# Five blocks of activations are turned by 32x32 stream transposes and a store and load, in place of TensorE transposes

## The chip, the cores and the metric

The kernel runs on one core of a Trainium2 chip. The metric is the device time of one execution in microseconds (us). The engines are named as in the profile: PE is TensorE (matmuls), PEld its weight loads, DVE is VectorE, ACT is ScalarE, POOL is GpSimd, SP is SyncE, which only issues DMAs. Each engine runs its own queue of instructions in a fixed order, and waits at an instruction until what it needs is there.

## The reference

A two-layer decoder trunk on 256 tokens of width 2048, all in float32. Layer 0 is a pooling mixer and a SwiGLU FFN; then one set of keys and values is made from the stream; layer 1 is attention over that set, and a SwiGLU FFN. Every sub-layer takes a normed and modulated stream. Cut to the two places that the change touches:

```python
def modulate(h, shift, scale):
    return h * (1.0 + scale[:, None, :]) + shift[:, None, :]
...
h = modulate(rmsnorm(x, norm_mix[1]), shift_m, scale_m)      # layer 1, the mixer's input
cq = rmsnorm(h @ w_dq, q_norm)                               # the queries' latent
q = (cq @ w_uq).reshape(B, S, N_HEADS, Q_HEAD_DIM)
...
x = x + gate_m[:, None, :] * y
h = modulate(rmsnorm(x, norm_ffn[1]), shift_f, scale_f)      # layer 1, the FFN's input
x = x + gate_f[:, None, :] * ((silu(h @ w_gate) * (h @ w_up)) @ w_down)
```

## The kernel before

**Products in three parts.** A float32 product is made from three matmuls of a reduced-precision type: each operand is split into an upper half (a rounded copy, ACT) and a lower half (the rest, by subtraction, DVE), and upper x upper, lower x upper and upper x lower are summed in PSUM. A weight unit is 512 x 512. `w_unit` (L384) loads it from DRAM on SP's queue into a `raw` buffer (six of them), and `split` (L372) makes its halves in two `hl` buffers (six): L376 on ACT, L378 on DVE. `proj_unit` (L412, its matmul is L422) multiplies one unit with one block of activations, for two groups of 128 tokens: 24 matmuls.

**Activations.** A block of activations is 512 channels of the normed, modulated stream for all 256 tokens, with the channels along the partitions, both halves in an `act` buffer. The stream itself (`x`) has tokens along the partitions, so a block has to be turned. `scaled` (L546) multiplies 512 columns of `x` by each token's reciprocal norm (ACT, L554), one piece for each group of 128 tokens. `turned_pieces` (L558) turns them by eight transposes on PE (L564) into two PSUM banks. `modulated` (L571) applies scale and shift, which are per channel and so per partition now: for each of four groups of 128 channels ACT writes the whole value (L582) and its upper half (L583), and DVE the lower half (L584). The pieces and the whole values lie in `t2k` buffers, of which there are seven.

**Background.** The modulation vectors come from products of a vector with large matrices. They are made on DVE in the background (`Part.unit`: a load of 1 MB on SP's queue, a multiply-and-sum L213), a few units at a time: `plan` and `release` set how many are to be done in a stage, and `tick`, called by each `split`, spreads them.

**The order.** Outside the stretches that are marked as ordered by hand, a planner sets each engine's queue when the kernel is built: work that is ready goes in the order of the program, and a later instruction goes first only where nothing earlier is ready on that engine. The two halves of a weight's split are given a priority as if they stood 100 instructions earlier; instructions under `urgent` (L588) go as early as they can. A buffer is given out when an instruction that writes it is placed.

**The queries' latent.** After FFN 0, keys and values are made in four groups (`keys_values`, L1367; `head_T`'s matmul is L1386). The pieces of the first block are scaled before group 1. In group 2, between its keys and its values, `last_of_background` (L1403) first places what is left of the stage's background and then calls `hidden_q` (L1396), which turns block 0, scales block 1 and modulates block 0. After group 2 `hidden_q` turns and modulates block 1. Blocks 2 and 3 need no turning: they were kept, turned, from the keys' and values' own norm. Then follow a few DVE additions that complete the rotary key (`rope_end`, L912, into `krT`, which GpSimd clears at L1413), the four units of `w_dq` with blocks 0 to 3 in that order, `Latent.norm` with a power on GpSimd (L1338), and group 3.

**The last FFN.** `start_ffn` (L930) begins the first six of eleven column chunks of both projections before all blocks are there: for each block j it runs over twelve units (six chunks, gate and up) with that block, for block 0 without the first two, which the handover from the attention has done. In the loop over the units, n counts 0 to 11; `pieces = ahead(j + 1)` scales the next block behind unit n = 7, and `hidden(j + 1, pieces)` turns and modulates it ahead of unit n = 11. Block 0 is made in the handover, blocks 1 to 3 in this way.

**An earlier use of the other way.** In both FFNs some chunks of the product of gate and up are already turned without PE: `turn_blocks` (L748) turns each 32x32 block in place (L752, a stream transpose on DVE) and stores the tile to DRAM (L754, on POOL's queue), and `transposed` (L764) loads it with partition and block index exchanged (L769, POOL's queue). What results has its channels in another order than PE's transpose gives, and the rows of the weights that meet it are laid out on the host in that order (`laid_out`, L1718).

Of the kernel before, what the change touches and what calls it, by code (L numbers as in the profile page):

```python
# [17 lines left out]
P = 128  # L18
# [77 lines left out]
def tile_trunk(ctx: ExitStack, tc: tile.TileContext, a: dict, out: bass.AP):  # L96
# [22 lines left out]
    def t2k(shape, dt=F32):  # L119
        return work.tile(shape, dt, tag="t2k", bufs=7, name=nm("t2k"))  # L120
# [437 lines left out]
    def turned_pieces(pieces):  # L558
# [7 lines left out]
            pts.append(pt)  # L566
        return pts

    mod_ins, hid_ins = [None], [None]

    def modulated(pts, j, c_scale, c_shift, direct=False):  # L571
        flush()
# [165 lines left out]
    def ffn(l, hT, gate_name, begun, then):  # L738
# [7 lines left out]
            return proj(ffn_weights(l)[which][:, c], hT)  # L746

        def turn_blocks(c):  # L748
            turned[c] = []
            for tok in range(NT):  # L750
                blocks = t2k([P, CH])
                dve.transpose(out=blocks, in_=nat[c][tok])  # L752
                rows = dram.tile([P, CH], F32, name=nm("turned"))
                pool.dma_start(rows, blocks)  # L754
                turned[c].append(rows)

        def turned_halves(m, tok, full):
            order = "p k (b j) -> p k b j"
# [5 lines left out]
        def transposed(c):  # L764
            m = act_t([P, 2, KL, T])
            if c in TURNED_BY_DMA[l]:
                for tok in range(NT):
                    full = t2k([P, CH])
                    pool.dma_start(full.rearrange("p (b e) -> p b e", e=P),  # L769
                                   turned[c][tok].rearrange("(b i) (g e) -> (i g) b e", i=BLOCK, e=P))  # L770
                    halves = lambda tok=tok, full=full: turned_halves(m, tok, full)
                    if c == GROUPS[-1][0]:
                        halves()
                    else:
                        pending.append((1, halves))
                mids[c] = m
                return
            for tok in range(NT):
                pt = ps_t()
                for f in range(KL):  # L780
                    pe.transpose(pt[:, f * P:(f + 1) * P], nat[c][tok][:, f * P:(f + 1) * P], ident)  # L781
                v = pt.rearrange("p (f t) -> p f t", f=KL)
                ts_ = slice(tok * P, (tok + 1) * P)
                act.activation(m[:, 0, :, ts_], v, AF.Copy)
                dve.tensor_tensor(out=m[:, 1, :, ts_], in0=v, in1=m[:, 0, :, ts_].bitcast(F32), op=ALU.subtract)
            mids[c] = m
# [143 lines left out]
    def start_ffn(l, first, ahead, hidden, late):  # L930
# [3 lines left out]
        with tc.issue_after(mod_ins[0].ins), tc.issue_after(hid_ins[0].ins) if hid_ins[0] else nullcontext():  # L934
            for j in range(ND - 1):
                if l == 0 and j == 1:
                    for tok in range(NT):
                        sync.dma_start(aside[0][:, tok], back[tok])
                todo = KD // 2 if j + 1 >= ND - late else 0
                for n, (c, which) in enumerate((c, w) for c in begun for w in (GATE, UP)):  # L940
                    if n == 2 * len(begun) - 1:
                        hT.append(hidden(j + 1, pieces))
                    if l == 0 or j > 0 or c > 0:
                        begun[c][which].block(j, hT[j])
                    if n == 2 * len(begun) - 5:
                        pieces = ahead(j + 1)
                    if todo and (n > 1 or j > 0 or l > 0):
                        pump(1)
                        todo -= 1
                pump(todo)  # L950
# [440 lines left out]
    with tc.issue_after(mod_ins[0].ins):  # L1391
        kv = [keys_values(0)]
    hmx = []
    pieces = scaled(rstd, 0)

    def hidden_q():  # L1396
        nonlocal pieces
        pts = turned_pieces(pieces) if len(hmx) < 2 else kept[len(hmx) - 2]
        if len(hmx) < 1:
            pieces = scaled(rstd, len(hmx) + 1)  # L1400
        hmx.append(modulated(pts, len(hmx), C_AM1, C_SM1))

    def last_of_background():  # L1403
        plan(n_all + MIX_DQ, 0)
# [253 lines left out]
    def first(pair):  # L1658
# [14 lines left out]
        with tc.manual_schedule(engines=ordered):  # L1673
# [28 lines left out]
            run(g1[0], g1[1], u1[0], u1[1], g1[2], u1[2])  # L1702
        return h.hT[0]

    hT, begun = start_ffn(1, first, lambda j: scaled(rstd, j),
                          lambda j, pieces: modulated(turned_pieces(pieces), j, C_AF1, C_SF1), LATE)
    plan(0, FFN1_UNITS)
    ffn(1, hT, "ffn1", begun, lambda: None)

# [5 lines left out]
    return w.reshape(k // CH, n // CH, P, KL * CH)  # L1715


def laid_out(i):  # L1718

    def columns(v):  # L1720
        return np.asarray(v).reshape(-1, P).T

    o = {n: np.asarray(i[n]) for n in ("x", "c", "positions", "mod_w", "final_norm")}
    o["vectors"] = np.concatenate([columns(i[n]) for n in (
        "c", "norm_mix", "norm_ffn", "kv_in_norm", "kv_norm", "q_norm", "pool_scale", "mod_b", "kv_mod_b")], 1)
    o["mod_wt"] = o["mod_w"].transpose(0, 2, 1)
    o["kv_mod_wt"] = np.asarray(i["kv_mod_w"]).T
    block = o["mod_w"][0].reshape(KD // 2, 2, P, 6, D)[:, :, :, 3:5, :CH]
    o["mod_block"] = block.transpose(0, 2, 1, 3, 4).reshape(KD // 2, P, 4 * CH)

# [6 lines left out]
    for n in ("w_dkv", "w_uk", "w_uv"):  # L1737
        o[n] = units(np.asarray(i[n]))
    o["pool_w"] = np.asarray(i["pool_w"])[0].reshape(-1, KL, P, CH).transpose(0, 2, 1, 3).reshape(-1, P, KL * CH)
    for n in ("w_dq", "w_o"):  # L1740
        o[n] = units(np.asarray(i[n])[0])
    for n in ("ffn_gate", "ffn_up", "ffn_down"):
        o[n] = np.stack([units(w) for w in np.asarray(i[n])])
    for l, chunks in enumerate(TURNED_BY_DMA):
        w = np.asarray(i["ffn_down"])[l].reshape(NF, KL, KL, BLOCK, ND, CH)[list(chunks)]
        o["ffn_down"][l, list(chunks)] = w.transpose(0, 4, 3, 1, 2, 5).reshape(len(chunks), ND, P, KL * CH)
    return o


# [16 lines left out]
```

## Time and profile before

| | us |
|---|---|
| timed, median of 3 | 1890.53 (1890.23 to 1890.56) |
| the profiled execution's own time | 1889.67 |
| its span, first to last instruction | 1887.9 |
| PE busy in the span | 1836.0 |
| DVE busy | 1431.6 |
| ACT busy | 836.2 |
| mean granted TensorE clock | 0.992 |

The span is the stretch that the trace covers, and the execution's own time has some 1.8 us more around it. Busy shares are averages over stages with different limits. The chain that ended last says which engine the end had to wait for, and a chain in order of time gives the price of a group on that path, while a mean duration of overlapping matmuls does not. Times in the views are us from the span's start; a row of a timeline holds the start, the length of the merged piece, engine, line and operation, what it writes and reads, and in brackets the idle time before it and what ended it.

### The profile page before, as it was taken

Reading aid. Unit: us, or ns where it says so; the run is one execution under the profiler, and the core shown is the slowest. Engines: PE = TensorE matmul, PEld = TensorE weight load, DVE = VectorE, ACT = ScalarE, POOL = GpSimd, SP = SyncE. Lnnn points to the kernel's source line nnn. Section 1 sums busy time; section 2 is a strip of 40 time slices with the busy share of each in tenths; the row PEclk is TensorE's granted clock in tenths of the full one; section 3 lists DMA queues with packets and bytes.
Section 4 is the critical chain, followed back from the end, with each engine's and each line's share of the span. In section 5 each row is a group of like instructions: output and inputs, shape, how many; then the busy total and the mean of one; then the engine's idle time right before and its main releaser. Section 6 shows DMA issues by size and latency. Waiting matters only on the chain.

```text
span 1887.9 us, 21743 instructions
## 1 busy us (share of the span) xinstructions
PE 1836.0 (97%) x8629; PEld 1489.2 (79%) x8629; DVE 1431.6 (76%) x1437; ACT 836.2 (44%) x914; POOL 56.1 (3%) x82
## 2 busy tenths in 40 slices
PE   6689999999999999999999999999999999999998
PEld 2356888888888888888889888888888888888886
DVE  1247799999889798897898886889778666645557
ACT  3125643453433334344776635634444433443343
POOL 0000000000000000000110000000011000000000
PEclk9889999999999999999999999999999999999999
DMA  9999998889999899995594485988788776766651
GB/s 399 415 420 411 387 365 335 322 311 367 406 350 420 346 407 390 392 420 205 200 376 166 168 342 199 386 328 333 264 312 318 293 268 237 267 253 235 223 200 45
DMA packets 84280, 589.14 MB, mean 312 GB/s; under 512 B 9761, under 2 KB 10193, under 8 KB 15441
## 3 DMA queue, kind: packets, MB, share of 16 engines
q1 hardware_dynamic: 79346, 570.68, 77.8%
q0 software_dynamic: 4592, 16.78, 2.4%
q8 instruction: 68, 1.11, 0.2%
q10 hardware_dynamic: 240, 0.29, 0.0%
q14 instruction: 34, 0.28, 0.0%
HBM read 574.58 MB, written 13.13 MB: 311 GB/s over the span
## 4 chain that ended last, share of the span: by engine, by line
PE 93%; DMA 5%; DVE 0%; ACT 0%; SPq 0%; issue 0%; POOLq 0%; DVEq 0%; ACTq 0%
PE ps L422 80%; DMA raw<-in_mod_w_dram 5%; PE ps L431 2%; PE ps L1033 2%; PE ps L1386 1%; PE ps L258 1%; PE ps L1472 1%; PE ps L1578 1%; PE ps L1289 1%; PE ps L781 0%; PE ps L564 0%; PE ps L1475 0%; DMA raw<-in_mod_block_dram 0%; PE ps L1487 0%; PE ps L1527 0%; PE ps L1488 0%
## 5 line engine op out<-in xcount | busy, mean ns | idle before, releaser
L422 PE MATMUL ps<-hl,act 128*128 128x512 f32 x6672 | 1518.5, 389 | 0.0
L422 PEld LDWEIGHTS ps<-hl,act 128*128 128x128 f32 x6672 | 1250.3, 188 | 260.2 <-ACT act L1108 0.9
L376 ACT ACTIVATE hl<-raw 128x2048 fp32r<-128x2048 f32 x285 | 545.8, 1918 | 638.2 <-PE ps L422 413.0
L378 DVE TENSOR_TENSOR hl<-raw,hl 128x2048 fp32r<-128x2048 f32 x285 | 651.3, 2287 | 196.6 <-ACT hl L376 196.5
L213 DVE SCALAR_TENSOR_TENSOR raw<-raw,s_row 128x2048 f32<-128x2048 f32 x168 | 383.1, 2284 | 15.5 <-DMA raw<-in_mod_wt_dram 15.4
L258 PE MATMUL ps<-raw,s_strip 128*32 128x512 f32 x392 | 59.0, 688 | 38.3 <-DMA raw<-in_mod_w_dram 37.9
L722 DVE TENSOR_TENSOR act<-ps,act 128x512 f32<-128x512 f32 x96 | 63.9, 682 | 15.4 <-PE ps L422 15.4
L258 PEld LDWEIGHTS ps<-raw,s_strip 128*32 128x32 f32 x392 | 8.8, 116 | 68.7 <-DMA raw<-in_mod_w_dram 47.6
L431 PE MATMUL ps<-hl,act 128*128 128x512 f32 x192 | 47.6, 400 | 0.6 <-DVE act L527 0.5
L431 PEld LDWEIGHTS ps<-hl,act 128*128 128x128 f32 x192 | 35.1, 188 | 10.3 <-ACT act L514 2.5
L794 DVE TENSOR_TENSOR x<-ps,x 128x512 f32<-128x512 f32 x32 | 21.6, 688 | 20.0 <-PE ps L422 20.0
L544 DVE TENSOR_TENSOR hl<-raw,hl 128x2048 fp32r<-128x2048 f32 (+3 forms) x17 | 31.9, 1879 | 4.8 <-ACT hl L541 4.7
L265 DVE COPY t2k<-ps 128x256 f32<-128x256 f32 x4 | 1.7, 425 | 44.3 <-ACT t2k L264 44.3
L1033 PEld LDWEIGHTS ps<-act,act 128*128 128x128 f32 x128 | 25.0, 202 | 11.7 <-issue 8.4
L754 POOL DMA_DIRECT2D turned<-t2k x26 | 14.5, 556 | 649.6 <-DVE t2k L752 649.3
L451 ACT ACTIVATE junk<-x 128x512 bf16<-128x512 f32 x23 | 14.5, 629 | 42.1 <-DVE x L636 25.0
L856 ACT ACTIVATE t2k<-ps 128x512 f32<-128x512 f32 x24 | 14.2, 592 | 41.8 <-PE ps L422 41.8
L1033 PE MATMUL ps<-act,act 128*128 128x256 f32 x128 | 32.4, 406 | 0.0
L720 ACT ACTIVATE act<-ps 128x512 f32<-128x512 f32 x32 | 19.1, 596 | 29.2 <-PE ps L422 29.2
L860 DVE TENSOR_TENSOR t2k<-ps,t2k 128x512 f32<-128x512 f32 x24 | 16.5, 687 | 19.9 <-PE ps L422 19.9
L541 ACT ACTIVATE hl<-raw 128x2048 fp32r<-128x2048 f32 (+1 forms) x15 | 26.5, 1766 | 3.5 <-PE ps L422 3.5
L998 DVE COPY hl<-ps 128x256 f32<-128x256 f32 x4 | 1.7, 423 | 30.4 <-PE ps L997 30.4
(235 smaller groups left out, 1044.3 us busy)
## 6 DMA issues: line engine op xcount, KB each, us to landing
raw<-in_mod_wt_dram SPq DMA_DIRECT2D x136, 1024.0 KB, 6.8
raw<-in_ffn_up_dram SPq DMA_DIRECT2D x88, 1024.0 KB, 6.5
raw<-in_ffn_down_dram SPq DMA_DIRECT2D x88, 1024.0 KB, 6.8
raw<-in_ffn_gate_dram SPq DMA_DIRECT2D x87, 1024.0 KB, 6.5
raw<-in_mod_w_dram SPq DMA_DIRECT2D x48, 1024.0 KB, 13.8
raw<-in_kv_mod_wt_dram SPq DMA_DIRECT2D x32, 1024.0 KB, 9.6
raw<-in_w_o_dram SPq DMA_DIRECT2D x16, 1024.0 KB, 5.4
raw<-in_mod_block_dram SPq DMA_DIRECT2D x8, 1024.0 KB, 12.5
```

The source lines that it names most:

```text
L213: dve.scalar_tensor_tensor(out=r, in0=r, scalar=1.0, in1=s_row, op0=ALU.mult, op1=ALU.mult, accum_out=self.sums[:, self.n:self.n + 1])
L258: pe.matmul(self.bank[m * STRIP:(m + 1) * STRIP, :], lhsT=weights(k), rhs=r[:, k, i, :], start=first, stop=last)
L376: hi_ins = act.activation(hi, r, AF.Copy)
L378: lo_ins = dve.tensor_tensor(out=lo, in0=r, in1=hi.bitcast(F32), op=ALU.subtract)
L422: pe.matmul(banks[tok], lhsT=t_[:, i, k, tok * P:(tok + 1) * P], rhs=w[:, k, :], start=first and n < len(part), stop=last and n >= len(ord ...
L431: pe.matmul(bank, lhsT=t_[:, i, k, tok * P:(tok + 1) * P], rhs=w[:, k, :], start=first and n == 0, stop=last and n == len(order) - 1)
L541: hid_ins[0] = act.activation(w[1], w[0], AF.Copy)
L544: dve.tensor_tensor(out=w[2][:, ks], in0=w[0][:, ks], in1=w[1][:, ks].bitcast(F32), op=ALU.subtract)
L720: act.activation(part, banks[tok], AF.Copy)
L722: dve.tensor_tensor(out=part, in0=banks[tok], in1=part, op=ALU.add)
L794: dve.tensor_tensor(out=sums, in0=bank, in1=sums, op=ALU.add)
L1033: pe.matmul(mixed[g][:, n % 2, :], lhsT=wp[g][:, k, ns], rhs=pool_all[g // 2][:, g % 2, k, :], start=k == 0, stop=k == KL - 1)
```

## The change

Blocks 0 and 1 of the queries' latent and blocks 1 to 3 of the last FFN go the way of `turn_blocks`. `turned_by_dma` takes the two scaled pieces of a block, turns their 32x32 blocks on DVE, stores each to DRAM, and loads them in four DMAs (two groups of tokens, two halves of 64 columns) into two tiles; each load has 128 x 4 pieces of 64 values, 256 bytes. `modulated_blocks` then makes the whole value and the halves as `modulated` does, reading the loaded tiles in SBUF instead of PSUM. The calls move: at the latent, block 0 is turned where it was only scaled, and block 1 is scaled, turned, stored and loaded behind block 0's modulation. In the last FFN the next block is asked for behind unit n = 3 instead of n = 7. `modulated` ran block 0 under `urgent`; `modulated_blocks` does not. `turn_blocks` and `transposed` now use the shared helpers, and do what they did. On the host, the rows of `w_dq`, of layer 1's gate and up weights, and the norm vectors, modulation weights and biases that belong to the turned blocks are laid out in the order of channels that this way gives.

```diff
--- before.py
+++ after.py
@@ -566,7 +566,40 @@
             pts.append(pt)
         return pts
 
+    def stored_blocks(pieces):
+        stored = []
+        for piece in pieces:
+            blocks = t2k([P, CH])
+            dve.transpose(out=blocks, in_=piece)
+            rows = dram.tile([P, CH], F32, name=nm("turned"))
+            pool.dma_start(rows, blocks)
+            stored.append(rows)
+        return stored
+
+    def channels_first(rows):
+        return rows.rearrange("(b i) (g e) -> (i g) b e", i=BLOCK, e=P)
+
+    def turned_by_dma(pieces):
+        stored = stored_blocks(pieces)
+        pairs = [t2k([P, NT * KL, 2 * BLOCK]) for _ in range(2)]
+        for tok in range(NT):
+            for h2 in range(2):
+                es = slice(2 * h2 * BLOCK, 2 * (h2 + 1) * BLOCK)
+                pool.dma_start(pairs[h2][:, tok * KL:(tok + 1) * KL, :], channels_first(stored[tok])[:, :, es])
+        return pairs
+
     mod_ins, hid_ins = [None], [None]
+
+    def modulated_blocks(pairs, j, c_scale, c_shift):
+        flush()
+        t_ = act_t([P, 2, KL, T])
+        for k in range(KL):
+            scale, bias = (cols[:, i, j * KL + k:j * KL + k + 1] for i in (c_scale, c_shift))
+            full, src = t2k([P, T]), pairs[k // 2][:, :, k % 2 * BLOCK:(k % 2 + 1) * BLOCK]
+            act.activation(full.rearrange("p (b j) -> p b j", j=BLOCK), src, AF.Identity, scale=scale, bias=bias)
+            act.activation(t_[:, 0, k, :], full, AF.Copy)
+            mod_ins[0] = dve.tensor_tensor(out=t_[:, 1, k, :], in0=full, in1=t_[:, 0, k, :].bitcast(F32), op=ALU.subtract)
+        return t_
 
     def modulated(pts, j, c_scale, c_shift, direct=False):
         flush()
@@ -746,13 +779,7 @@
             return proj(ffn_weights(l)[which][:, c], hT)
 
         def turn_blocks(c):
-            turned[c] = []
-            for tok in range(NT):
-                blocks = t2k([P, CH])
-                dve.transpose(out=blocks, in_=nat[c][tok])
-                rows = dram.tile([P, CH], F32, name=nm("turned"))
-                pool.dma_start(rows, blocks)
-                turned[c].append(rows)
+            turned[c] = stored_blocks(nat[c])
 
         def turned_halves(m, tok, full):
             order = "p k (b j) -> p k b j"
@@ -766,8 +793,7 @@
             if c in TURNED_BY_DMA[l]:
                 for tok in range(NT):
                     full = t2k([P, CH])
-                    pool.dma_start(full.rearrange("p (b e) -> p b e", e=P),
-                                   turned[c][tok].rearrange("(b i) (g e) -> (i g) b e", i=BLOCK, e=P))
+                    pool.dma_start(full.rearrange("p (b e) -> p b e", e=P), channels_first(turned[c][tok]))
                     halves = lambda tok=tok, full=full: turned_halves(m, tok, full)
                     if c == GROUPS[-1][0]:
                         halves()
@@ -942,7 +968,7 @@
                         hT.append(hidden(j + 1, pieces))
                     if l == 0 or j > 0 or c > 0:
                         begun[c][which].block(j, hT[j])
-                    if n == 2 * len(begun) - 5:
+                    if n == 2 * len(begun) - (9 if l == DEPTH - 1 else 5):
                         pieces = ahead(j + 1)
                     if todo and (n > 1 or j > 0 or l > 0):
                         pump(1)
@@ -1391,14 +1417,14 @@
     with tc.issue_after(mod_ins[0].ins):
         kv = [keys_values(0)]
     hmx = []
-    pieces = scaled(rstd, 0)
+    pairs = turned_by_dma(scaled(rstd, 0))
 
     def hidden_q():
-        nonlocal pieces
-        pts = turned_pieces(pieces) if len(hmx) < 2 else kept[len(hmx) - 2]
-        if len(hmx) < 1:
-            pieces = scaled(rstd, len(hmx) + 1)
-        hmx.append(modulated(pts, len(hmx), C_AM1, C_SM1))
+        nonlocal pairs
+        j = len(hmx)
+        hmx.append(modulated_blocks(pairs, j, C_AM1, C_SM1) if j < 2 else modulated(kept[j - 2], j, C_AM1, C_SM1))
+        if j == 0:
+            pairs = turned_by_dma(scaled(rstd, 1))
 
     def last_of_background():
         plan(n_all + MIX_DQ, 0)
@@ -1702,8 +1728,8 @@
             run(g1[0], g1[1], u1[0], u1[1], g1[2], u1[2])
         return h.hT[0]
 
-    hT, begun = start_ffn(1, first, lambda j: scaled(rstd, j),
-                          lambda j, pieces: modulated(turned_pieces(pieces), j, C_AF1, C_SF1), LATE)
+    hT, begun = start_ffn(1, first, lambda j: turned_by_dma(scaled(rstd, j)),
+                          lambda j, pairs: modulated_blocks(pairs, j, C_AF1, C_SF1), LATE)
     plan(0, FFN1_UNITS)
     ffn(1, hT, "ffn1", begun, lambda: None)
 
@@ -1715,16 +1741,31 @@
     return w.reshape(k // CH, n // CH, P, KL * CH)
 
 
+def by_blocks(v, blocks):
+
+    o, n = np.array(v), [CH * b + r for b in blocks for r in range(CH)]
+    w = o[n].reshape((len(blocks), KL, KL, BLOCK) + o.shape[1:])
+    o[n] = w.transpose((0, 2, 3, 1) + tuple(range(4, w.ndim))).reshape((-1,) + o.shape[1:])
+    return o
+
+
 def laid_out(i):
 
     def columns(v):
         return np.asarray(v).reshape(-1, P).T
 
-    o = {n: np.asarray(i[n]) for n in ("x", "c", "positions", "mod_w", "final_norm")}
+    i = {n: np.asarray(v) for n, v in i.items()}
+    o = {n: i[n] for n in ("x", "c", "positions", "mod_w", "final_norm")}
+    early, late = range(2), range(1, ND)
+    turned = [g * ND + j for gs, js in (((0, 1), early), ((3, 4), late)) for g in gs for j in js]
+    last = [by_blocks(m, turned) for m in (i["mod_w"][1].T, i["mod_b"][1])]
+    i["norm_mix"] = np.stack([i["norm_mix"][0], by_blocks(i["norm_mix"][1], early)])
+    i["mod_b"] = np.stack([i["mod_b"][0], last[1]])
+    i["norm_ffn"] = np.stack([i["norm_ffn"][0], by_blocks(i["norm_ffn"][1], late)])
     o["vectors"] = np.concatenate([columns(i[n]) for n in (
         "c", "norm_mix", "norm_ffn", "kv_in_norm", "kv_norm", "q_norm", "pool_scale", "mod_b", "kv_mod_b")], 1)
-    o["mod_wt"] = o["mod_w"].transpose(0, 2, 1)
-    o["kv_mod_wt"] = np.asarray(i["kv_mod_w"]).T
+    o["mod_wt"] = np.stack([i["mod_w"][0].T, last[0]])
+    o["kv_mod_wt"] = i["kv_mod_w"].T
     block = o["mod_w"][0].reshape(KD // 2, 2, P, 6, D)[:, :, :, 3:5, :CH]
     o["mod_block"] = block.transpose(0, 2, 1, 3, 4).reshape(KD // 2, P, 4 * CH)
 
@@ -1737,13 +1778,11 @@
     for n in ("w_dkv", "w_uk", "w_uv"):
         o[n] = units(np.asarray(i[n]))
     o["pool_w"] = np.asarray(i["pool_w"])[0].reshape(-1, KL, P, CH).transpose(0, 2, 1, 3).reshape(-1, P, KL * CH)
-    for n in ("w_dq", "w_o"):
-        o[n] = units(np.asarray(i[n])[0])
-    for n in ("ffn_gate", "ffn_up", "ffn_down"):
-        o[n] = np.stack([units(w) for w in np.asarray(i[n])])
-    for l, chunks in enumerate(TURNED_BY_DMA):
-        w = np.asarray(i["ffn_down"])[l].reshape(NF, KL, KL, BLOCK, ND, CH)[list(chunks)]
-        o["ffn_down"][l, list(chunks)] = w.transpose(0, 4, 3, 1, 2, 5).reshape(len(chunks), ND, P, KL * CH)
+    o["w_dq"] = units(by_blocks(i["w_dq"][0], early))
+    o["w_o"] = units(i["w_o"][0])
+    for n in ("ffn_gate", "ffn_up"):
+        o[n] = np.stack([units(i[n][0]), units(by_blocks(i[n][1], late))])
+    o["ffn_down"] = np.stack([units(by_blocks(w, chunks)) for w, chunks in zip(i["ffn_down"], TURNED_BY_DMA)])
     return o
 
 
```

## The prediction

> **What bounds the kernel now.** I read the page first (busy shares, then the chain that ended last), then the chain in order of time around the two places that the change touches, then the busy time by stage, and last the order on VectorE and GpSimd there.
>
> The page's shares, its chain, and the one row of the transposes that the change is about:
>
> ```profile
> PE 1836.0 (97%) x8629; PEld 1489.2 (79%) x8629; DVE 1431.6 (76%) x1437; ACT 836.2 (44%) x914; POOL 56.1 (3%) x82
> PE 93%; DMA 5%; DVE 0%; ACT 0%; SPq 0%; issue 0%; POOLq 0%; DVEq 0%; ACTq 0%
> L564 PE MATMUL ps<-con,t2k 128*128 128x128 f32 x72 | 9.5, 272 | 0.0
> ```
>
> TensorE is the bound: it holds 93% of the chain, and nothing else but the loads of the first stage has a share. L564 is the transpose in turned_pieces, 72 times: nine blocks of eight. The mean of 272 ns is not its price, since matmuls overlap; the chain in order of time (start, length, what) has the price:
>
> ```profile
> 955.75 0.87 PE ps L564 x8
> 956.62 5.49 PE ps L422 x24
> 962.12 0.87 PE ps L564 x8
> 962.99 21.78 PE ps L422 x96
> 984.76 5.75 PE ps L1386 x48
> ...
> 1217.10 0.87 PE ps L564 x8
> 1217.97 65.30 PE ps L422 x288
> 1283.28 0.87 PE ps L564 x8
> 1284.15 65.30 PE ps L422 x288
> 1349.45 0.87 PE ps L564 x8
> ```
>
> A block of eight costs 0.87 us on the path, and the five blocks that the change takes away all stand there: two before the queries' latent (955.75, 962.12), three at the start of the last FFN. In both places matmuls stand directly before and after. So **the ceiling of the gain is 5 x 0.87 = 4.35 us** (2.61 in the FFN, 1.74 at the latent).
>
> How full the rest is, by stage (us, then PE, PEld, DVE, ACT, POOL busy, granted clock, DMA share, GB/s):
>
> ```profile
> 935.00:957.00 22.00, 22.00 (x148) 20.32 (x147) 21.93 (x19) 14.00 (x17) 0.00 (x0) 1.00 0.99 392
> 957.00:985.00 28.00, 28.00 (x131) 23.30 (x130) 28.00 (x33) 22.51 (x43) 0.76 (x1) 1.00 0.96 381
> 1168.00:1197.00 29.00, 29.00 (x130) 23.95 (x129) 28.25 (x22) 15.42 (x16) 0.00 (x0) 1.00 0.98 395
> 1197.00:1217.00 20.00, 20.00 (x90) 16.52 (x89) 13.67 (x8) 12.95 (x13) 0.00 (x0) 1.00 0.96 381
> 1217.00:1283.00 66.00, 66.00 (x297) 54.80 (x296) 56.95 (x54) 28.49 (x26) 0.00 (x0) 1.00 0.90 333
> 1283.00:1350.00 67.00, 67.00 (x305) 55.62 (x304) 57.15 (x54) 28.13 (x23) 0.00 (x0) 1.00 0.81 303
> ```
>
> The two places differ. In the FFN's start VectorE has 6 to 10 us free before each block is due. Before the latent VectorE is full from 935 to 985, and the DMA engines are at 0.96 to 0.99: what the change adds there joins two queues without a gap.
>
> **The change, part by part.** Prices of what is added or replaced:
>
> ```profile
> L752 DVE STREAM_TRANSPOSE t2k<-t2k 128x512 f32<-128x512 f32 x26 | 17.8, 698 | 7.9 <-DMA turned<-t2k 7.7
> L754 POOL DMA_DIRECT2D turned<-t2k x26 | 14.5, 556 | 649.6 <-DVE t2k L752 649.3 <-issue 0.2
> L769 POOL DMA_DIRECT2D t2k<-turned x26 | 19.9, 766 | 141.7 <-issue 82.8 <-DVE act L762 27.7 <-DMA turned<-t2k 22.6
> L582 ACT ACTIVATE t2k<-act,cols 128x256 f32<-128x256 f32 x8 | 4.5, 600 | 0.0
> L582 ACT ACTIVATE t2k<-ps,cols 128x256 f32<-128x256 f32 x20 | 10.1, 560 | 0.0
> L583 ACT ACTIVATE act<-t2k 128x256 fp32r<-128x256 f32 x28 | 10.2, 418 | 0.0
> ```
>
> Per block it adds two VectorE turns (2 x 0.70 = 1.40 us), two stores (GpSimd 0.56 each) and four loads of half the size of L769's (0.77 each, taken whole, since each still has 512 pieces). ScalarE reads SBUF instead of PSUM: 0.60 for 0.56, four times, +0.16, in stages where it is 42 to 80% busy. Five blocks cost VectorE 7.0 us and the DMA engines 5 x 1.05 = 5.2 MB. What the layout change on the host moves costs nothing on the chip: same bytes, same shapes.
>
> *The FFN's start.* A block is now asked for after unit 3 of twelve and used after unit 11: eight units of 65.30 / 12 = 5.44 us, 43.5 us of lead. The trip, with the slowest landing of the whole run (10.5, below) twice: 1.3 scaling + 1.4 + 1.1 issue + 10.5 + 3.1 issue + 10.5 = 28 us. It is hidden. VectorE's 1.40 fits its 6 to 10 free us. The DMA engines need 1.05 MB / 0.389 MB per us = 2.7 us a block; only the first block meets a stage with no such room (0.98 and 0.96). What covers it is the lead of the weights (engine, what it waited for, us in total, times, longest; 1168 to 1350):
>
> ```profile
> ACT hl L376 <- PE ps L422: 75.1, 23, 4.4
> ACT hl L376 <- DMA raw<-in_ffn_up_dram: 1.5, 1, 1.5
> ```
>
> ScalarE's splits wait for TensorE to free a buffer, 75 us, and for a load 1.5. If that cover fails in the first block, it costs up to the 2.7 us once; I take 0. **FFN: -2.61 us.**
>
> *The latent.* Here the second block's lead is short. TensorE without waits would begin the first unit of w_dq at 962.99 - 1.74 = 961.25 and the second, which needs the second block, 21.78 / 4 = 5.44 later, at 966.7. When does VectorE turn that block? ScalarE has it scaled early (L554, second row); VectorE's queue around it and the one GpSimd row that L912 depends on:
>
> ```profile
> 185.83 0.53 POOL L1413 MEMSET krT<- 128x512 f32 x1 [25.39 <-DVE t2k L1098]
> 934.56 0.43 DVE L907 TENSOR_TENSOR t2k<-ps,cos_t 128x256 f32<-128x256 f32 x1
> 935.39 1.33 ACT L554 ACTIVATE t2k<-x,rstd 128x512 f32<-128x512 f32 x2
> 937.09 1.33 ACT L554 ACTIVATE t2k<-x,rstd 128x512 f32<-128x512 f32 x2
> 937.11 2.29 DVE L378 TENSOR_TENSOR hl<-raw,hl 128x2048 fp32r<-128x2048 f32 x1
> 952.57 2.29 DVE L378 TENSOR_TENSOR hl<-raw,hl 128x2048 fp32r<-128x2048 f32 x1
> 954.77 1.70 DVE L912 TENSOR_TENSOR krT<-t2k 32x256 f32<-32x256 f32 x4
> 984.25 2.46 POOL L1338 TENSOR_TENSOR sm<-sm,mhalf 128x1 f32<-128x1 f32 x1 [61.81 <-DVE sm L1337]
> ```
>
> L912 has all its inputs at 935.0 (L907 and the memset) and runs at 954.77: work that stands late in the program waits 20 us, until everything ahead of it that is ready has gone. The second block's turns stand in the program a little before L912, behind all background sums of this stage and within reach of the next units' splits, which have priority. So I put them where L912 stands, later by the first block's 1.40: 956.17 to 957.57. The stage's own landings (first row: stores, second: a load; the third is the range of all 52) come from the one place before where the DMA engines were as full, 0.98:
>
> ```profile
> 546.00:560.00 14.00, 14.00 (x64) 11.58 (x63) 13.96 (x11) 3.84 (x2) 1.88 (x3) 1.00 0.98 376
> DMA to landing us min/median/max: 5.4/5.4/5.5
> DMA to landing us min/median/max: 7.3/7.3/7.3
> DMA to landing us min/median/max: 2.3/5.8/10.5
> ```
>
> Stores issued at 956.87 and 957.57, landed 0.56 + 5.4 later: 962.8 and 963.5. GpSimd waits for the first and issues four loads of 0.77 each from 962.9; the third, which completes the first pair, is out at 965.2. Its landing is not in the trace at this size; nearest rows 5.4 and 7.3, I take the middle, 6.4: 971.6. ScalarE then makes two columns in 2 x (0.60 + 0.42), with overlap 1.8, and two more: 975.2. The unit's eight products with the upper half, 8 x 0.227, were over at 968.44 + 1.81 = 970.25 before; now at 975.2 + 0.45 = 975.65. **Latent: +5.4 us** against before, a wait of about 7 in TensorE's queue. Queued behind the wait: on ScalarE the splits of the next units, on GpSimd the powers of L1338, not due before 984; on TensorE everything. The first block, turned from 937.11 + 2.2 = 939.3 (after the split that starts as its pieces are scaled), arrives by the same steps near 955 and is in time.
>
> Bounds of this part: with no wait -1.74; with the longest landing (10.5) for store and load +5.4 + 5.1 + 4.1 = +14.6.
>
> **Sum**: -2.61 + 5.4 = +2.8 on the profiled execution's 1889.67 us (span 1887.9 and 1.8 around it), 1892.5. The timed median, 1890.53, lies 0.86 above that execution, so 1893.3.
>
> The Trainium skill's page "DMA: Bandwidth & Descriptors" (Specifications) speaks against the loads: under 512 B a piece no longer moves at line rate, and these have 256 B. No run here shows it yet; if the half loads therefore land as late as whole ones (7.3), the sum is 1894.2.
>
> **Rivals.**
> *All hidden* (faster). If VectorE gets the second block soon after 938.4, when it is scaled, or the trip is short, the block is there before 966.7 and the whole 4.35 comes through: 1886.2. For it: ScalarE's early L554, and landings down to 2.3. Against it: L912's 20 us, and 0.99 DMA share. The same page's fit (Anatomy of one DMA — SWDGE (gpsimd) path), 2.0 us plus bytes over 436 GB/s, gives 2.6 for a store and 2.3 for a half load, which is this rival even with the late turn, 1886.4 by estimate. The trace's 5.4 to 7.7 in a full stage disagree with it.
>
> *Buffers* (slower). t2k has seven buffers. At 955 the key rope's, two scaled pieces, two pairs and the first block's whole columns can hold all; the second block's turns then wait for the first block's subtractions, which come behind the split of a further unit and the first block's own columns. That is 4 us or more later: 1897 to 1902. It decides from 1 us of further delay, where the sum passes +3.8. For it: two new kinds of tile share the seven. Against it: stored pieces are given back near 952.
>
> *Half of it.* VectorE finds a gap for the second block some 4 to 5 us earlier (a load late, a split not ready), and the wait eats only the latent's gain or a little more: about 1889 to 1891, no change.
>
> **How the numbers follow.** What a measurement can tell from no change is about 0.2%, 3.8 us. Forecast 0.45: its own range is +0.5 to +6, a bit over a third of it (0.17) beyond +3.8, the rest (0.28) within. All hidden 0.25 (0.04 of it by the short trip), buffers 0.20, half 0.10. Faster 0.25; same 0.28 + 0.10, with 0.02 of the buffers' case = 0.40; slower 0.35. Eight in ten: from the full gain, 1886.0, to 1899.5, which leaves out the worst third of the buffers' case and the longest landings.
>
> **What would show it.** 40 of the 72 L564 gone, and L422 running through 1217, 1283 and 1349 without a break: the FFN's part. For the latent: the second pair of stream transposes starting near 956 (forecast), before 945 (all hidden) or after 959 (buffers); their stores to landing near 5 or 2; and a gap in TensorE before the second unit of w_dq, with ScalarE waiting on a load of the turned rows. I am wrong in the FFN if a gap opens near 1180 with splits waiting for weights, and at the latent if L912's place says nothing of the new turns'.

## The result and the profile after

| | before | after |
|---|---|---|
| timed, median (lowest to highest), us | 1890.23 (1889.82 to 1890.56) | 1920.11 (1918.34 to 1922.44) |
| the profiled execution's own time, us | 1889.67 | 1919.56 |
| its span, us | 1887.9 | 1917.4 |
| mean granted TensorE clock | 0.992 | 0.980 |

After to before is 1.0156, 95% interval 1.0145 to 1.0167. The change costs 29.9 us. The forecast was 1893.3, within 1886.0 to 1899.5: the time lies far outside.

First the page of after, its busy shares and its chain by engine:

```profile
PE 1843.8 (96%) x8589; PEld 1492.2 (78%) x8589; DVE 1437.4 (75%) x1447; ACT 836.1 (44%) x914; POOL 76.7 (4%) x112
PE 88%; DMA 6%; issue 2%; DVE 2%; ACT 1%; POOL 0%; SPq 0%; POOLq 0%; DVEq 0%; ACTq 0%
```

TensorE has 40 instructions fewer, as announced, and yet it is busy 7.8 us longer. It holds 88% of the chain and not 93%; "issue" has 2% and VectorE and ScalarE 3% where all three had 0. Line numbers have moved by the new lines: the stores are L575, the new loads L588, the whole values and upper halves of `modulated_blocks` L599 and L600, `scaled` is still L554. Next, TensorE's waits (engine, line, what it waited for: us in total, times, longest):

```profile
PE ps L422 <- ACT act L600: 23.3, 3, 12.9
PE ps L422 <- ACT hl L376: 3.2, 1, 3.2
```

L422 had no wait at all before; now it has 26.5 us. The first row is the latent, the second the last FFN, as TensorE's timeline of after shows:

```profile
969.78 8.14 PE L422 MATMUL ps<-hl,act 128*128 128x512 f32 x24 [9.59 <-ACT act L600]
990.78 2.07 PE L422 MATMUL ps<-hl,act 128*128 128x512 f32 x4 [12.86 <-ACT act L600]
993.68 15.42 PE L422 MATMUL ps<-hl,act 128*128 128x512 f32 x56 [0.82 <-ACT act L600]
...
1195.04 38.24 PE L422 MATMUL ps<-hl,act 128*128 128x512 f32 x168
1236.43 183.94 PE L422 MATMUL ps<-hl,act 128*128 128x512 f32 x803 [3.15 <-ACT hl L376]
```

The lengths count as well as the waits. At the 0.227 us a matmul of the prediction's 288 in 65.30 us, 24, 4 and 56 of them take 5.44, 0.91 and 12.70 us. Here they take 8.14, 2.07 and 15.42: 6.6 us more in all, right behind the waits. The windows of these stretches have the reason (us, then busy time of PE, PEld, DVE, ACT, POOL, granted clock, DMA share, GB/s):

```profile
957.00:985.00 28.00, 11.33 (x39) 8.51 (x37) 13.40 (x15) 12.34 (x18) 4.90 (x7) 0.76 0.61 223
985.00:1010.00 25.00, 18.40 (x67) 14.48 (x68) 18.41 (x23) 15.44 (x27) 0.75 (x1) 0.72 0.61 226
1237.00:1300.00 63.00, 63.00 (x272) 51.82 (x271) 55.25 (x50) 33.62 (x36) 4.15 (x6) 0.97 0.91 348
```

The granted clock is 0.76 and 0.72 at the latent and 0.97 behind the FFN's wait, where it was 1.00 before. **The account of the 29.5 us of span**: the latent 23.3 (waits) + 6.6 (slower clock) - 1.7 (transposes gone) = 28.2; the FFN 3.15 + some 1.6 (803 matmuls take 182.3 us at 0.227, here 183.9) - 2.6 = 2.1; together 30.3. The first stages, which the change does not touch, took 1.0 us less in this execution (L1386, now L1412, begins group 2 at 925.68 and not at 926.69), which leaves 29.3.

Why is the block late? GpSimd's timeline of after, from the first store of the latent to its last load, and the first three loads of the FFN:

```profile
939.33 0.63 POOL L575 DMA_DIRECT2D turned<-t2k  x1 [17.91 <-DVE t2k L573]
947.75 0.77 POOL L588 DMA_DIRECT2D t2k<-turned  x1 [7.79 <-DMA turned<-t2k]
948.52 0.56 POOL L575 DMA_DIRECT2D turned<-t2k  x1
954.82 0.76 POOL L588 DMA_DIRECT2D t2k<-turned  x1 [5.74 <-PE ps L1412]
961.81 0.75 POOL L588 DMA_DIRECT2D t2k<-turned  x1 [6.24 <-issue]
...
972.32 1.15 POOL L575 DMA_DIRECT2D turned<-t2k  x2 [6.75 <-DVE t2k L573]
...
989.53 0.75 POOL L588 DMA_DIRECT2D t2k<-turned  x1 [6.09 <-issue]
...
1213.72 0.76 POOL L588 DMA_DIRECT2D t2k<-turned  x1 [6.20 <-DMA turned<-t2k]
1220.15 0.77 POOL L588 DMA_DIRECT2D t2k<-turned  x1 [5.67 <-PE ps L422]
1227.05 0.75 POOL L588 DMA_DIRECT2D t2k<-turned  x1 [6.14 <-issue]
...
```

Two things stand here. The four loads of a block do not follow each other: up to 7 us lie between two of them, and most of that is put down to "issue", which is idle time that no semaphore of the trace explains. And the second store, whose tile VectorE had turned at 941.8, stands in the queue behind the first load and goes out at 948.52. ScalarE's timeline of after shows what that does to others:

```profile
964.59 0.60 ACT L599 ACTIVATE t2k<-t2k,cols 128x256 f32<-128x256 f32 x1 [15.18 <-DMA t2k<-turned]
965.10 1.89 ACT L376 ACTIVATE hl<-raw 128x2048 fp32r<-128x2048 f32 x1
...
970.55 1.33 ACT L554 ACTIVATE t2k<-x,rstd 128x512 f32<-128x512 f32 x2
...
989.34 1.09 ACT L599 ACTIVATE t2k<-t2k,cols 128x256 f32<-128x256 f32 x2 [12.41 <-DMA t2k<-turned]
...
1233.49 1.09 ACT L599 ACTIVATE t2k<-t2k,cols 128x256 f32<-128x256 f32 x2 [7.74 <-DMA t2k<-turned]
1234.49 1.89 ACT L376 ACTIVATE hl<-raw 128x2048 fp32r<-128x2048 f32 x1
```

ScalarE stands for 15 us at the first value of block 0. Behind it stand a weight split (L376) and the scaling of block 1 (L554 at 970.55; before it was done at 937.09), so block 1's whole trip begins 33 us late and TensorE waits a second time. In the FFN the same queue holds the split that TensorE needs at 1236.43.

### The profile page after: what moved, and what is told of

The parts are those of the page before. It is cut to its first block, busy times and chain, and to the rows that moved or that the text cites. A ratio compares the mean times of both kernels' runs of the same rounds, so it can differ in the third digit from the quotient of the medians.

```text
span 1917.4 us, 21740 instructions
## 1 busy us (share of the span) xinstructions
PE 1843.8 (96%) x8589; PEld 1492.2 (78%) x8589; DVE 1437.4 (75%) x1447; ACT 836.1 (44%) x914; POOL 76.7 (4%) x112
## 4 chain that ended last, share of the span: by engine, by line
PE 88%; DMA 6%; issue 2%; DVE 2%; ACT 1%; POOL 0%; SPq 0%; POOLq 0%; DVEq 0%; ACTq 0%
PE ps L422 76%; DMA raw<-in_mod_w_dram 4%; PE ps L431 2%; PE ps L1059 2%; PE ps L258 2%; DMA turned<-t2k 1%; PE ps L1498 1%; PE ps L1604 1%; DVE hl L378 1%; DMA t2k<-turned 1%; PE ps L1315 1%; ACT hl L376 0%; PE ps L807 0%; PE ps L1501 0%; DMA raw<-in_mod_block_dram 0%
## 5 line engine op out<-in xcount | busy, mean ns | idle before, releaser
L422 PE MATMUL ps<-hl,act 128*128 128x512 f32 x6672 | 1526.0, 391 | 26.4 <-ACT act L600 23.3
L422 PEld LDWEIGHTS ps<-hl,act 128*128 128x128 f32 x6672 | 1255.9, 189 | 290.0 <-ACT act L600 24.8
L376 ACT ACTIVATE hl<-raw 128x2048 fp32r<-128x2048 f32 x285 | 545.6, 1917 | 617.9 <-PE ps L422 374.5
L378 DVE TENSOR_TENSOR hl<-raw,hl 128x2048 fp32r<-128x2048 f32 x285 | 651.2, 2287 | 218.3 <-ACT hl L376 217.8
L213 DVE SCALAR_TENSOR_TENSOR raw<-raw,s_row 128x2048 f32<-128x2048 f32 x168 | 383.0, 2284 | 12.9 <-DMA raw<-in_mod_wt_dram 12.8
L575 POOL DMA_DIRECT2D turned<-t2k x36 | 20.1, 559 | 596.1 <-DVE t2k L573 595.8
L599 ACT ACTIVATE t2k<-t2k,cols 128x256 f32<-128x256 f32 x20 | 11.0, 592 | 49.5 <-DMA t2k<-turned 38.7
L573 DVE STREAM_TRANSPOSE t2k<-t2k 128x512 f32<-128x512 f32 x36 | 24.6, 699 | 7.2 <-DMA turned<-t2k 6.5
## 6 DMA issues: line engine op xcount, KB each, us to landing
raw<-in_mod_w_dram SPq DMA_DIRECT2D x48, 1024.0 KB, 12.9
```

What stands on the lines that cost most here:

```text
L213: dve.scalar_tensor_tensor(out=r, in0=r, scalar=1.0, in1=s_row, op0=ALU.mult, op1=ALU.mult, accum_out=self.sums[:, self.n:self.n + 1])
L376: hi_ins = act.activation(hi, r, AF.Copy)
L378: lo_ins = dve.tensor_tensor(out=lo, in0=r, in1=hi.bitcast(F32), op=ALU.subtract)
L422: pe.matmul(banks[tok], lhsT=t_[:, i, k, tok * P:(tok + 1) * P], rhs=w[:, k, :], start=first and n < len(part), stop=last and n >= len(ord ...
L573: dve.transpose(out=blocks, in_=piece)
```

## The experiments

Theory Q of the expectations: GpSimd writes the descriptors of its DMAs into a space of a fixed size, set to 1024 bytes in this kernel; a load of 512 pieces fills it, so that the next load waits until the one before has gone. Its rivals stand in each expectation.

**More room, after's code.** The order of the instructions on every engine is that of after.

```diff
-    nc = bacc.Bacc("TRN2", target_bir_lowering=False, num_devices=1, dynamic_dma_scratch_size=1024)
+    nc = bacc.Bacc("TRN2", target_bir_lowering=False, num_devices=1, dynamic_dma_scratch_size=4096)
```

> The changed kernel with 4096 bytes per partition in place of 1024 for the descriptors of GpSimd's DMAs; every engine's order is the same. Theory Q (room in the queue): a load of 512 pieces fills the room, so each of a block's loads is issued only when the one ahead has landed (in the changed kernel they stand 7.1, 7.0 and 3.0 us apart at 947.8, and 6.4, 6.9 and 6.6 at 1213.7, with GpSimd idle between them and waiting for nothing that the profile shows). With room they follow each other in 0.8 us where their stores are in, TensorE's waits of 9.6 and 12.9 us at the latent shrink to some 4 and 5, the one of 3.2 us in the FFN goes, and the time falls from 1920 to between 1900 and 1907. Theory R (slow transfers): the pieces of 256 bytes on full DMA engines take that long themselves, room or not: 1918 to 1922. Theory S (late start): what counts is that the second block is scaled only at 970.6, behind the first one's modulation: within 3 us of 1920.

Measured: 1906.05 us (1904.88 to 1907.68), 1.0086 of before (1.0069 to 1.0103). GpSimd's timeline of this run:

```profile
948.75 0.56 POOL L575 DMA_DIRECT2D turned<-t2k  x1
949.29 0.75 POOL L588 DMA_DIRECT2D t2k<-turned  x1
958.13 1.49 POOL L588 DMA_DIRECT2D t2k<-turned  x2 [8.09 <-DMA turned<-t2k]
...
975.63 3.11 POOL L588 DMA_DIRECT2D t2k<-turned  x4 [2.16 <-ACT act L1404]
...
1204.64 3.02 POOL L588 DMA_DIRECT2D t2k<-turned  x4 [6.17 <-DMA turned<-t2k]
```

Four loads now go out in 3.1 us, as the prediction had reckoned, and no "issue" is left. Some 14 of the 29.9 us go with it: Q holds, and the rivals R and S fall as sole causes. The rest stays: the second store still goes out behind the first load (948.75), the loads of its rows wait for it until 958.13, block 1 is still scaled at 970.55, and TensorE still waits twice, 7.5 and 6.3 us. So the room took half of the second wait (12.9 us in after) and all of the FFN's, but only 2.1 us of the first (9.6), whose block waits for its second store.

**More room, the kernel before.** The same edit, as a control.

> Control: the kernel before with 4096 in place of 1024 bytes for the descriptors. Its loads of turned tiles wait for each other too (82.8 us of idle GpSimd put down to nothing), but no engine on the path waits for them: all theories expect 1890.2 within 1 us.

Measured: 1890.05 us, 1.0002 of before (0.9993 to 1.0012): no change. But the row that the prediction quoted for the price of a load, here by line in this run, has lost its 82.8 us of "issue":

```profile
L769 POOL DMA_DIRECT2D t2k<-turned x26 | 19.7, 760 | 106.0 <-DMA turned<-t2k 52.9 <-DVE act L762 47.7 <-PE ps L422 5.0
```

So the same wait was in the kernel before, where nobody waited for those loads. The idle time as a whole fell only from 141.7 to 106.0 us, since other waits then come last (52.9 us for stores, 47.7 for VectorE).

**One place alone.** The FFN's three blocks with the latent as before, and the latent's two with the FFN as before, both with 1024 bytes. The edits at the call, without what they undo on the host; the latent alone also asks for the FFN's blocks behind n = 7 again:

```diff
-    pairs = turned_by_dma(scaled(rstd, 0))
+    pieces = scaled(rstd, 0)
...
+        pts = turned_pieces(pieces) if len(hmx) < 2 else kept[len(hmx) - 2]
```

```diff
-    hT, begun = start_ffn(1, first, lambda j: turned_by_dma(scaled(rstd, j)),
+    hT, begun = start_ffn(1, first, lambda j: scaled(rstd, j),
...
```

> Only the three blocks of the last FFN go through DRAM; the latent's are turned by TensorE as before; room for descriptors as in the change (1024). From the two traces the FFN's start comes 27.0 us later and the end 29.5: its share should be +2.5 us, 1892.7 (Q and R, since neither frees the loads). As the prediction had it: -2.6, 1887.6.

> Only the two blocks of the queries' latent go through DRAM; the last FFN as before. From the two traces: +27 to +28 us, 1917 to 1918 (Q, R and S). As the prediction had it: +5.4, 1895.6.

Measured: the FFN alone 1892.05 us, 1.0012 (1.0003 to 1.0022); the latent alone 1916.72, 1.0142 (1.0127 to 1.0157). By these ratios they cost 2.3 and 26.8 us, together 29.1 of the 29.9: within the intervals the two places add up. And the FFN, for which -2.61 was forecast, loses.

**The FFN with room.** The FFN alone, 4096 bytes.

> Only the FFN's three blocks through DRAM, with 4096 bytes for GpSimd's descriptors. Theory Q (room in the queue): the four loads of a block go out together, ScalarE no longer stands at the first block's values ahead of a weight's split, and the whole 3 x 0.87 = 2.6 us come through: 1887.1 to 1887.6. Theory R (slow transfers): as with 1024, 1892. Theory A (ScalarE's order alone): as with 1024.

Measured: 1886.91 us (1886.14 to 1888.88), 0.9984 (0.9975 to 0.9993). That is 3.4 us less than before, and the forecast's 2.61 is inside the interval (1.3 to 4.7 us). TensorE's timeline of this run has one unbroken piece, where the kernel before is broken three times by transposes (1217.10, 1283.28 and 1349.45):

```profile
1167.66 262.71 PE L422 MATMUL ps<-hl,act 128*128 128x512 f32 x1158
```

**The FFN without room, another order on ScalarE.** What did TensorE wait for in the FFN, the loads or the split behind ScalarE's wait? Here the loads stay one at a time (1024 bytes), but a block's values are placed behind the last weight split that stands ahead of them in the program.

```diff
+            hi_ins = last_upper[0] = act.activation(hi, r, AF.Copy)
...
+    def behind_splits(j, pairs):
+        with tc.issue_after(last_upper[0].ins):
+            return modulated_blocks(pairs, j, C_AF1, C_SF1)
...
-                          lambda j, pairs: modulated_blocks(pairs, j, C_AF1, C_SF1), LATE)
+                          behind_splits, LATE)
```

> Only the FFN's three blocks, 1024 bytes, but a block's values are placed on ScalarE's queue behind the upper half of the last weight split that stands ahead of them in the program. Theory A (what holds TensorE in the FFN is the weight's split behind ScalarE's wait, not the block itself): the wait of 3.2 us goes although the loads are as late as before, 1887 to 1888. If the block itself comes too late: 1891 or more.

Measured: 1887.25 us (1886.39 to 1890.02), 0.9987 (0.9978 to 0.9996). First, from the run with the FFN alone and 1024 bytes, ScalarE's timeline; then GpSimd's, ScalarE's and TensorE's timelines of this run (its L590, L601, L378 and L424 are L588, L599, L376 and L422, two lines further):

```profile
1205.91 1.09 ACT L599 ACTIVATE t2k<-t2k,cols 128x256 f32<-128x256 f32 x2 [7.14 <-DMA t2k<-turned]
1206.90 1.89 ACT L376 ACTIVATE hl<-raw 128x2048 fp32r<-128x2048 f32 x1
```

```profile
1206.04 0.75 POOL L590 DMA_DIRECT2D t2k<-turned  x1 [5.90 <-issue]
```

```profile
1200.84 1.91 ACT L378 ACTIVATE hl<-raw 128x2048 fp32r<-128x2048 f32 x1
...
1203.56 1.91 ACT L378 ACTIVATE hl<-raw 128x2048 fp32r<-128x2048 f32 x1
1205.84 0.60 ACT L601 ACTIVATE t2k<-t2k,cols 128x256 f32<-128x256 f32 x1 [0.37 <-DMA t2k<-turned]
```

```profile
1167.45 252.72 PE L424 MATMUL ps<-hl,act 128*128 128x512 f32 x1114
```

The last load goes out at 1206.04, as late as in the FFN alone (1206.11), and TensorE no longer waits: two splits go by while the block is still on its way. The loads were late, but in the FFN the lateness reached TensorE only through ScalarE's queue.

**Both mendings at once** (the edit just shown, and 4096 bytes).

> The three blocks of the FFN alone, with both mendings: 4096 bytes for GpSimd's descriptors, and a block's values placed on ScalarE's queue behind the last split. Either of them alone gave 1886.9 and 1887.3 us. If each removes the same wait, as theory Q has it, the two together give no more than one: 1886.4 to 1887.6, and TensorE's row of L422 unbroken from the first to the last unit of the FFN's start. If they remove different waits, up to 0.5 us less, below 1886.4.

Measured: 1887.20 us (1886.47 to 1889.90), 0.9986 (0.9976 to 0.9995). No more than either alone: they remove the same wait.

**Fewer, larger loads.** After with two loads of 256 KB a block, in pieces of 512 bytes, in place of four of 128 KB in pieces of 256. A load still has 512 pieces. ScalarE makes the whole value of each column group in two halves, which the lines below leave out.

```diff
-        pairs = [t2k([P, NT * KL, 2 * BLOCK]) for _ in range(2)]
+        pairs = [t2k([P, KL, P]) for _ in range(NT)]
         for tok in range(NT):
...
+            pool.dma_start(pairs[tok], channels_first(stored[tok]))
...
```

> The changed kernel with 1024 bytes for the descriptors as it is, but each block loaded by two DMAs of 256 KB in pieces of 512 bytes, in place of four of 128 KB in pieces of 256; ScalarE makes each column group in two halves. Same bytes, half the loads, and 512 pieces in each as before. Theory Q: two waits for room fewer in each block, of some 6 us: the first block 2 us earlier (its second store lands late anyway), the second some 9: 1905 to 1911. Theory R, if the pieces of 256 bytes are what is slow: the loads land sooner, also below 1912, but those of 256 KB would then stand closer to each other than 5 us without waiting for a store; by Q they do not. If bytes on full DMA engines are what counts: 1918 to 1922.

Measured: 1911.41 us (1909.62 to 1914.05), 1.0115 (1.0101 to 1.0129), 0.4 us beyond what Q gave and far from the theory of bytes. GpSimd's timeline of this run has this row for the latent's second block:

```profile
982.75 0.76 POOL L586 DMA_DIRECT2D t2k<-turned  x1 [5.61 <-issue]
```

The second load waits as long as with small pieces. So what counts is the number of loads, not the size of their pieces: two loads have one such wait where four have three. Nor do these loads, of twice the bytes, land sooner or much later (5.4 to 7.8 us, median 6.9; in after 2.7 to 7.3, median 6.5). Every load in these runs had 512 pieces, so that the pieces are what fills the room is not shown; a store, of 128 rows, goes out directly behind a load even with 1024 bytes (948.52).

**How much room.** After with 2048 bytes.

> The changed kernel with the room for GpSimd's descriptors set to 2048 bytes, twice what it has (with 1024: 1920.1 us, loads one at a time; with 4096: 1906.1 us, loads back to back). Theory Q (room by proportion): if one load of 512 pieces fills 1024 bytes, two fit here. At the second block of the latent the first pair of loads then goes out at once and the second pair one landing, 6 to 7 us, later; the unit's wait is up to that much longer than with 4096, and the FFN's third load, due near 1211, is early enough. 1909 to 1914 us, and the loads in pairs or in threes. Rival (a threshold: any room above one load is enough): 1905 to 1908, all four back to back. Rival (the descriptors' room has nothing to do with it and 4096 moved something else): near 1920.

Measured: 1904.97 us (1904.07 to 1907.01), 1.0080 (1.0066 to 1.0094). The time is that of 4096 bytes, just below the threshold's range and 4 us below that by proportion. But the loads do not all go at once, as GpSimd's timeline shows:

```profile
1204.30 2.27 POOL L588 DMA_DIRECT2D t2k<-turned  x3 [6.08 <-DMA turned<-t2k]
1210.86 0.75 POOL L588 DMA_DIRECT2D t2k<-turned  x1 [4.30 <-issue]
```

Three fit into 2048 bytes where, in after, one fits into 1024. The room acts in steps of whole loads; my "two by proportion" was wrong, and the fourth load's 4.3 us hurt nobody. Why it is three is not settled.

**The latent asked for early, with room.** Both blocks are scaled, turned and stored ahead of group 1, with 4096 bytes, so that block 1 no longer stands behind block 0's values.

```diff
-    pairs = turned_by_dma(scaled(rstd, 0))
+    pairs = [turned_by_dma(scaled(rstd, j)) for j in range(2)]
...
-        if j == 0:
-            pairs = turned_by_dma(scaled(rstd, 1))
```

> The changed kernel with 4096 bytes for the descriptors, and both blocks of the latent scaled, turned, stored and loaded ahead of group 1 (the second no longer behind the first one's modulation). Theory S (late start, what is left at 1906): the second block is turned some 26 us earlier, TensorE's second wait (6.3 us) goes and the first (7.5) shrinks, since the second store is issued ahead of the first load; 1889 to 1895. If the start counts for nothing: 1906.

Measured: 1896.36 us (1894.07 to 1899.35), 1.0035 (1.0022 to 1.0049): 9.7 less than with room alone, but a little above the range expected, and still 9.45 more than the FFN alone with room. TensorE's waits between 930 and 1300 in this run, then in the second fence VectorE's timeline:

```profile
PE ps L422 <- ACT act L600: 2.5, 1, 2.5
PE ps L294 <- DVE cols L302: 2.1, 1, 2.1
PE ps L564 <- DVE t2k L1365: 1.7, 1, 1.7
PE ps L422 <- DVE act L601: 1.1, 1, 1.1
```

```profile
946.99 0.71 DVE L573 STREAM_TRANSPOSE t2k<-t2k 128x512 f32<-128x512 f32 x1 [2.48 <-DMA turned<-t2k]
```

Four waits of 7.4 us are left, three of them for VectorE, which is 87 to 93% busy from 960 to 1010, and block 1's two turns stand 2.48 and 0.94 us, the first of them shown, until stores give back `t2k` buffers. So an early start saves most, but not enough: the latent has no cover for this trip. With 1.7 us of slow clock behind the first of them and less the 1.74 of the transposes this makes 7.4; the profiled executions lie 8.2 us apart. What share each of VectorE's work, the buffers and the full DMA engines has in these 7.4 us was not taken apart.

## Why the prediction was wrong

**The ceiling was right.** 5 x 0.87 = 4.35 us: the 40 transposes are gone, and the FFN's part of it, 2.61, comes through in the three kernels with the FFN alone and no wait there (3.4, 3.0 and 3.3 us, with intervals from 0.8 to 4.7).

**The step that failed is the price of the loads.** "Four loads of half the size of L769's (0.77 each, taken whole ...)" put them 0.77 us apart, at the latent as in the FFN's "3.1 issue". In after they are 3 to 7.6 us apart, because one fills the space for descriptors. The row on which this rested hinted at it: 141.7 us of idle time, with "issue 82.8" first. The duration was read and the idle time beside it was not, although 82.8 / 26 = 3.2 us a load was there to be seen. With room the steps are 0.77 apart, and 14 us go. A second step failed beside it, the early start of the latent's second block (below): mending that too takes another 9.7 us, and 6.1 us over the kernel before (1890.26 beside that run) are left. The Trainium skill's page "DMA: Bandwidth & Descriptors" (SWDGE vs HWDGE vs iDMA) says that GpSimd appends these descriptors to rings in a part of SBUF set aside for them; the runs agree with a place of limited size.

**The FFN's "It is hidden ... I take 0" was wrong by a step of its own.** The trip was compared with the lead up to the block's use (28 against 43.5 us). TensorE met its effect earlier than that use: the values are placed on ScalarE's queue ahead of a split, and the split is what TensorE waited for (3.15 us, then some 1.6 of slow clock in this execution). The list of what is queued behind was made for the latent and not for the FFN. There the sign named was a gap "with splits waiting for weights"; the gap came, with a split waiting in line.

**The latent: +5.4 forecast, some +28 measured.** After's chain in order of time (start, length, what) goes step by step past the prediction's:

```profile
939.33 7.77 DMA turned<-t2k
...
948.52 7.81 DMA turned<-t2k
956.33 5.49 issue
961.81 2.70 DMA t2k<-turned
...
979.27 3.42 issue
...
983.45 6.09 issue
989.53 2.67 DMA t2k<-turned
```

The landings taken were not the fault: a store and a load were put at 5.4 + 6.4 = 11.8, and are 7.8 + 2.7 = 10.5 here; all 20 new loads landed in 2.7 to 7.3 us, median 6.5. What was missed is that the two stores of the first block go one after the other, with a load between them in GpSimd's queue, and the 5.49, 3.42 and 6.09 us of "issue". That the first block "arrives by the same steps near 955 and is in time" fell with it: its first value is made at 964.59. L912's place as the sign for the second block's turns fell too, not because VectorE was later but because ScalarE, which had scaled that block at 937.09, now does so at 970.55 behind block 0's values. The 937.09 was read from the kernel before, where `hidden_q` scales block 1 ahead of block 0's modulation; the diff puts it behind, so this could be seen beforehand. The prediction named the splits behind the wait, but not this scaling, which is itself the start of the next trip: the wait fed itself.

The Trainium skill's fit on the page "DMA: Bandwidth & Descriptors" (Anatomy of one DMA — SWDGE (gpsimd) path), 2.6 us for a store and 2.3 for a half load by estimate, which stood behind "all hidden", is near the two loads' 2.70 and 2.67 here, for which the DMA engines had room (share 0.44 at most in any microsecond of theirs). It is a third of the stores' 7.8, which fell into a stretch at 0.99, and of the new loads' median of 6.5.

**What was not in the sum at all** is TensorE's clock: 6.6 us at the latent, some 1.6 in the FFN.

**The rivals.** None is what happened. The one that ends slower, the seven `t2k` buffers, does not hold TensorE in after; its wait appears (3.4 us) only where both blocks are asked for at once. "All hidden" is true of the FFN, given room or the other order.

## What to carry to other kernels

When a queue's row has much idle time "issue" that no semaphore explains, ask what the engine itself runs out of before charging its busy time; loads of 512 pieces on GpSimd needed room for their descriptors here, and the sign was there while nobody waited for them. Test it by giving room, since not every such row means this: with both mendings and 4096 bytes a load still shows 6.91 us of "issue" (at 1226.81), directly behind the store whose rows it reads; the stores of that run land in 2.3 to 8.3 us. When a value comes by DMA instead of from an engine, list what stands behind its first reader on that engine, and look above all for the step that starts the next trip. Of this change the FFN's part is worth keeping, with more room or with the values behind the splits (1886.9 to 1887.3 us, the fastest times here); the latent's is not.

## What the hardware showed

**A wait of TensorE can cost more than its length.** The windows of after around the latent's first wait (columns as above, the clock third from the end):

```profile
964.00:966.00 2.00, 0.00 (x0) 0.00 (x0) 0.00 (x0) 1.41 (x2) 0.76 (x1) 0.68 0.02 4
...
974.00:975.00 1.00, 1.00 (x3) 0.78 (x3) 0.81 (x1) 1.00 (x3) 0.00 (x0) 0.53 0.88 328
975.00:976.00 1.00, 1.00 (x6) 0.81 (x5) 1.00 (x1) 1.00 (x2) 0.54 (x1) 1.00 0.01 0
```

TensorE's last matmul ended at 960.2. The clock falls to 0.50 some 4.5 us later (0.68 over two microseconds is 1.00 up to 964.7) and is back at 974.9, 5.2 us after work began again at 969.78: three matmuls in a microsecond, then six. 5.2 us at half the clock are 2.6 us lost. Even the FFN's wait of 3.15 us was followed by such a stretch, which cost the 1.6 us above, and the one of 2.52 us with the latent asked early (0.50 from 966 to 969). But the same FFN wait in the run with the FFN alone, 3.23 us, was not: the clock there is 1.00 throughout (1205 to 1216). The length alone doesn't decide it; what does is not shown here. The Trainium skill's page "TensorE: Matmul & The Clock Gate" (What's actually happening) has the clock halved after an idle window of about 3.4 us and released after about as long of work; the two values of the clock agree (1.00 and 0.50), but the release took 5 us here, and waits of 3.15 and 2.52 us could be enough.

**Room for descriptors goes by whole loads**: of 512 pieces one at a time with 1024 bytes, three with 2048, at least four with 4096, and a load that finds none waits for the one before, 2.3 to 6.9 us in after.
